# One level of Strassen in both float32 feed-forward products of two token groups, up and down as separate phases

## The chip, the cores and the metric

One core of one Trainium2 chip runs the whole layer. The metric is the device time of one execution in microseconds (us), as the median over runs. The engines are called as in the profile: PE (matmuls; PEld loads its weights), DVE (VectorE), ACT (ScalarE), POOL (GpSimd) and SP, which issues the DMAs here.

## The reference

One layer of a streaming encoder over 1024 prompt rows and 64 sample rows, width 1024, hidden width 4096, all in float32. Cut to what matters:

```python
u2 = x1 * (1.0 + sc2) + sh2
f = jnp.square(jax.nn.relu(u2 @ w['w_up'] + w['b_up'])) @ w['w_down'] + w['b_down']
y = _ln(ALPHA * x1 + (1.0 + g2) * f, w['ln2_g'], w['ln2_b'])
```

Ahead of it stand a conditioned input product, a recurrence, a band attention, an output product and LN1, which gives `x1`.

## The kernel before

The 1088 rows (tokens) are the columns of all tiles, in three groups of 384, 384 and 320. A float32 product is made of three matmuls (`mm3`, L101): each operand is split into a high part, which ACT copies out, and a low part, which DVE subtracts (`wsplit` L83 for weights, `split` L93 for activations); the three are high by high, high by low, low by high. The program has these stages in order: the conditioning and the input `u`; eight heads; the output product and LN1 with the activations `u2h`, `u2l` of each group (L526 to L592); the feed-forward and LN2 (L594 to L710).

The feed-forward goes in eight chunks of four blocks of 128 hidden columns (f-blocks). `up` (L617) loads and splits one 512 KB weight block and makes the three groups' hidden tiles: 24 matmuls a group, `relu` and square on ACT (L607, L608), high and low part on DVE (L609, L610), in SBUF. `down` (L625) takes the four f-blocks of the chunk for one group: eight output blocks of 12 matmuls, and one DVE operation each that adds the PSUM result into `facc` (L635), which lies in SBUF for all groups and was begun in LN1 by POOL (L576). In the last chunk `final` (L637) of a group comes right behind its `down`: transposes back to rows, statistics, normalisation on ACT (L650), multiplication by `lg` on DVE (L652), addition of `lb` on POOL (L653), and the output (L654).

The order of each engine's instructions is set by a scheduler that works from the program's order and a timeline it keeps itself; each engine then runs its own list in order. All DMAs are issued by SP, in its order, and one that waits for a buffer holds those behind it. The weights' raw and split tiles (`wraw`, `whi`, `wlo`) have three buffers each.

Of the kernel before, what the change touches and what calls it, by code (L numbers as in the profile page):

```python
# [47 lines left out]
def body(nc, tc, a):  # L48
    V, S, G, TE, SY = nc.vector, nc.scalar, nc.gpsimd, nc.tensor, nc.sync
    with ExitStack() as es:  # L50
        cpool = es.enter_context(tc.tile_pool(name="const", bufs=1))
# [49 lines left out]
        def mm3(ps, wh, wl, xh, xl, first, last):  # L101
            TE.matmul(ps, wh, xh, start=first, stop=False)  # L102
            TE.matmul(ps, wh, xl, start=False, stop=False)  # L103
            TE.matmul(ps, wl, xh, start=False, stop=last)  # L104

        # ------------------------------------------------ conditioning and u
# [454 lines left out]
        def ln1_b(g, n1, c, cw):  # L561
# [11 lines left out]
            for fb in range(NB):  # L573
                if fb not in facc:
                    facc[fb] = big([P, T], f"facc{fb}")
                G.tensor_scalar(facc[fb][:, t0 + c:t0 + c + cw], nT[:, fb, :], sA[:, fb:fb + 1], bA[:, fb, w:w + 1],  # L576
                                op0=ALU.mult, op1=ALU.add)
# [34 lines left out]
        def up_w(f):  # L612
            return wsplit(a["w_up"][f], f"u{f}")
# [163 lines left out]
```

## Time and profile before

| | us |
|---|---|
| median of three runs (1808.9 to 1810.18) | 1809.67 |
| span of the profiled execution, first to last instruction (the page has no other time of it) | 1807.1 |
| PE busy, 11032 matmuls | 1771.4 |
| DVE busy | 888.7 |
| ACT busy | 611.9 |
| POOL busy | 167.4 |

Times count from the start of the span. Busy times of different engines lie beside each other; a group of instructions has a total, a mean in ns and, behind the bar, the idle time that its engine had just before them, with what ended it. Matmuls are pipelined, so one lasts longer in its row than the distance to the next.

### The profile page before, as it was taken

The page shows a single profiled execution, that of the slowest core. Times are in us where ns is not written, and L with a number is a line of the kernel's source. Part 1 is how long each engine was busy: PE and PEld are TensorE (multiplying, and loading weights), DVE is VectorE, ACT ScalarE, POOL GpSimd, SP SyncE. Part 2 cuts the span into 40 slices and gives each one's busy share as a digit, 9 for nine tenths or more (in the row PEclk, how much of TensorE's full clock was granted, in tenths as well). Part 3 has the DMA queues.
Part 4 walks back from the last instruction along what each step waited for, and adds up shares of the span by engine and source line. Part 5 has one row for each costly group of instructions (what it writes and reads, how often), then busy time and mean ns, then how long its engine had stood idle before and what let it go on. Part 6 is the DMA issues. An engine that isn't in the chain of part 4 may idle for free.

```text
span 1807.1 us, 26471 instructions
## 1 busy us (share of the span) xinstructions
PE 1771.4 (98%) x11032; PEld 1738.7 (96%) x11032; DVE 888.7 (49%) x1707; ACT 611.9 (34%) x981; POOL 167.4 (9%) x243
## 2 busy tenths in 40 slices
PE   7999999999999999999999999999999999999995
PEld 4999999999999999999999999999999999999995
DVE  5594553637455374653657742424242434333447
ACT  2452534526244362533534531313130312121232
POOL 1100010000001000010027620000000000000004
PEclk9999999999999999999999999999999999999998
DMA  9231213112121212212264220202020202020102
GB/s 363 92 119 57 96 55 105 54 61 92 67 98 49 91 62 72 77 67 76 79 192 150 66 71 12 82 12 83 12 80 15 70 24 71 15 69 24 57 15 99
DMA packets 50711, 137.84 MB, mean 76 GB/s; under 512 B 6752, under 2 KB 18272, under 8 KB 50592
## 3 DMA queue, kind: packets, MB, share of 16 engines
q1 hardware_dynamic: 50592, 136.16, 22.0%
q8 instruction: 86, 1.41, 0.3%
q14 instruction: 33, 0.27, 0.0%
HBM read 123.03 MB, written 13.11 MB: 75 GB/s over the span
## 4 chain that ended last, share of the span: by engine, by line
PE 94%; DVE 2%; POOL 2%; DMA 1%; issue 1%; ACT 0%; SPq 0%; ACTq 0%; POOLq 0%; DVEq 0%
PE z L104 12%; PE z L103 12%; PE z L102 12%; PE up L104 7%; PE up L102 7%; PE up L103 7%; PE dn L102 7%; PE dn L104 7%; PE dn L103 7%; PE po L395 3%; PE s L384 2%; PE pt L389 1%; PE op L104 1%; PE op L102 1%; PE op L103 1%; POOL facc L576 1%
## 5 line engine op out<-in xcount | busy, mean ns | idle before, releaser
L102 PE MATMUL z<-uh,wh_in 128*128 128x384 f32 (+1 forms) x1320 | 435.5, 330 | 2.9 <-ACT uh L95 2.9
L103 PE MATMUL z<-ul,wh_in 128*128 128x384 f32 (+1 forms) x1320 | 436.8, 331 | 0.3 <-DVE ul L96 0.3
L104 PE MATMUL z<-uh,wl_in 128*128 128x384 f32 (+1 forms) x1320 | 435.7, 330 | 0.0
L635 DVE SCALAR_TENSOR_TENSOR facc<-dn,ada,facc 128x384 f32<-128x384 f32 (+2 forms) x256 | 122.1, 498 | 310.2 <-PE dn L104 310.1
L102 PE MATMUL dn<-hh,wh_d 128*128 128x384 f32 (+1 forms) x768 | 253.9, 331 | 3.8 <-DVE facc L635 3.7
L102 PEld LDWEIGHTS z<-uh,wh_in 128*128 128x128 f32 x1320 | 248.7, 188 | 6.3 <-ACT uh L95 3.9
L102 PE MATMUL up<-u2h,wh_u 128*128 128x384 f32 (+1 forms) x768 | 251.1, 328 | 2.0 <-ACT u2h L95 2.0
L103 PEld LDWEIGHTS z<-ul,wh_in 128*128 128x128 f32 x1320 | 248.6, 188 | 4.4 <-DVE ul L96 2.3
L104 PEld LDWEIGHTS z<-uh,wl_in 128*128 128x128 f32 x1320 | 248.5, 188 | 4.0 <-issue 3.1
L104 PE MATMUL dn<-hh,wl_d 128*128 128x384 f32 (+1 forms) x768 | 251.8, 328 | 0.0
L103 PE MATMUL dn<-hl,wh_d 128*128 128x384 f32 (+1 forms) x768 | 251.7, 328 | 0.0
L103 PE MATMUL up<-u2l,wh_u 128*128 128x384 f32 (+1 forms) x768 | 251.3, 328 | 0.0
L104 PE MATMUL up<-u2h,wl_u 128*128 128x384 f32 (+1 forms) x768 | 244.3, 328 | 0.0
L607 ACT ACTIVATE h<-up,bup 128x384 f32<-128x384 f32 (+1 forms) x96 | 53.4, 556 | 356.3 <-PE up L104 356.3
L102 PEld LDWEIGHTS dn<-hh,wh_d 128*128 128x128 f32 x768 | 144.1, 188 | 5.0 <-DVE facc L635 4.3
L102 PEld LDWEIGHTS up<-u2h,wh_u 128*128 128x128 f32 x768 | 144.5, 188 | 2.3 <-ACT u2h L95 2.3
L104 PEld LDWEIGHTS up<-u2h,wl_u 128*128 128x128 f32 x768 | 144.0, 188 | 1.4 <-DVE wl_u L90 1.4
L103 PEld LDWEIGHTS up<-u2l,wh_u 128*128 128x128 f32 x768 | 144.8, 188 | 0.0
L103 PEld LDWEIGHTS dn<-hl,wh_d 128*128 128x128 f32 x768 | 144.4, 188 | 0.0
L104 PEld LDWEIGHTS dn<-hh,wl_d 128*128 128x128 f32 x768 | 144.2, 188 | 0.0
L89 ACT ACTIVATE wh_in<-wr_in 128x1024 fp32r<-128x1024 f32 x56 | 59.4, 1060 | 105.2 <-PE z L103 100.3
L90 DVE TENSOR_TENSOR wl_in<-wr_in,wh_in 128x1024 fp32r<-128x1024 f32 x56 | 68.5, 1223 | 43.2 <-ACT wh_in L89 43.0
(237 smaller groups left out, 2379.2 us busy)
## 6 DMA issues: line engine op xcount, KB each, us to landing
wr_in<-in_w_in SPq DMA_DIRECT2D x56, 512.0 KB, 3.3
ar<-in_w_ada SPq DMA_DIRECT2D x46, 512.0 KB, 5.0
wr_u<-in_w_up SPq DMA_DIRECT2D x33, 512.0 KB, 3.3
wr_d<-in_w_down SPq DMA_DIRECT2D x32, 512.0 KB, 3.9
wr_o<-in_w_out SPq DMA_DIRECT2D x24, 512.0 KB, 3.3
xT<-in_xT SPq DMA_DIRECT2D x8, 544.0 KB, 8.7
out_y<-y SPq DMA_DIRECT2D x8, 512.0 KB, 2.6
mg_d<-gl SPq DMA_DIRECT2D x7, 544.0 KB, 2.7
```

Of the source, the lines that this page charges most:

```text
L89: S.activation(hi, raw, AF.Copy)
L90: V.tensor_tensor(lo, raw, hi.bitcast(F32), op=ALU.subtract)
L102: TE.matmul(ps, wh, xh, start=first, stop=False)
L103: TE.matmul(ps, wh, xl, start=False, stop=False)
L104: TE.matmul(ps, wl, xh, start=False, stop=last)
L384: TE.matmul(sps[:, bk, :cw], qq[:, q0:q0 + P], kk[:, P * j0 + c0:P * j0 + c0 + cw], start=(ip == 0), stop=(ip == 2))
L389: TE.transpose(pt[:, P * j:P * j + P] if j < 4 else po[:, P:2 * P], pr[:, P * j:P * j + P], ident)
L395: TE.matmul(po[:, :P], v[:, j0 + j, :], pts[:, P * j:P * j + P], start=(j == 0), stop=(j == nk - 1))
L576: G.tensor_scalar(facc[fb][:, t0 + c:t0 + c + cw], nT[:, fb, :], sA[:, fb:fb + 1], bA[:, fb, w:w + 1], op0=ALU.mult, op1=ALU.add)
L607: S.activation(h1[:, :tw], ps[:, :tw], AF.Relu, bias=bup[:, f:f + 1])
L635: V.scalar_tensor_tensor(fc, ps[:, c0:c1], ada[:, G2, fb, w:w + 1], fc, op0=ALU.mult, op1=ALU.add)
```

## The change

The 2x2 block form of a product (two row halves of the weights' output, two halves of the contraction, groups 0 and 1 as the two column halves) takes seven products of quarter size in place of eight, with sums of weights and sums of activations as operands. An f-block is paired with the one four further on, 16 pairs in all.

The first two pairs are still made plainly, during LN1 of group 2. For pairs 2 to 15 `wops` loads both weight blocks, makes four sums of 128x512 on POOL and splits the blocks and the sums; `strassen` makes 84 matmuls of 128x384 for the seven products, with each of the three PSUM tiles x, y, z shared by products; `after` adds the tiles up on DVE and applies relu and square on ACT. The activation sums T1 to T4 are made once, on DVE. Group 2 stays plain (`up_g2`); for the last four pairs it is made behind all the Strassen products, with the weights loaded again. `put_pair` makes four sums of each pair's hidden tiles on POOL and writes seven operands to DRAM (`hs_d`), and group 2's tiles go to `hg_d`. The start of `facc` goes to `facc_d` in DRAM, from LN1.

The down phase then has, for each of four chunks, seven operands of 128x1536 (786 KB) loaded (two raw buffers) and split, and four blocks of two output blocks each, 84 matmuls, whose seven products go straight from PSUM into `facc` on DVE. Behind it stand group 2's down products in two halves (r = 0 and 1) of four output blocks, with the weights loaded again, `final` of groups 0 and 1 between the halves, and `final` of group 2 at the end. `w_down` lies in another layout in DRAM.

The diff, cut to its core:

```diff
-        fs = range(c, c + CH)
...
-            for g in range(3):
-                down(fs, ws, g)
-                if c == NFF - CH:
-                    final(g)
+        def put_pair(p, c11, c12, c21, c22, g2s, new_t):
+            c, i = divmod(p, 4)
+            t1, t2, t3, t4 = (new_t(f"t{p}_{k}") for k in range(4))
+            G.tensor_tensor(t1, c12, c11, op=ALU.subtract)
+            G.tensor_tensor(t2, c22, t1, op=ALU.subtract)
+            G.tensor_tensor(t3, c22, c12, op=ALU.subtract)
+            G.tensor_tensor(t4, c21, t2, op=ALU.subtract)
+            for k, src in enumerate((c11, c21, t2, t1, t3, c22, t4)):
+                SY.dma_start(hs_d[c, k][:, i, :], src)
...
+        for q in range(2):
+            k2 = slice(2 * q, 2 * q + 2)
+            x, y, z = (fp.tile([P, 2, GW], F32, tag="tt", bufs=3, name=f"tt{q}_{k}") for k in range(3))
...
+            join(x, b11)
+            join(y, b12)
+            join(z, b22)
+            V.tensor_tensor(x, y, x, op=ALU.subtract)
+            V.tensor_tensor(y, z, y, op=ALU.subtract)
+            V.tensor_tensor(z, z, x, op=ALU.subtract)
+            tsplit(2, z)
+            tsplit(1, x)
+            join(x, b21)
+            tsplit(3, y)
+            V.tensor_tensor(x, x, z, op=ALU.subtract)
+            tsplit(4, x)
+        uops = [b11, b21, ut[2], ut[1], ut[3], b22, ut[4]]
...
+            split(*wa, ra)
+            G.tensor_tensor(s1, rb[:, h[0], :], rb[:, h[1], :], op=ALU.add)
+            G.tensor_tensor(s2, s1, ra[:, h[0], :], op=ALU.subtract)
+            split(*sums[0], sr[0])
+            G.tensor_tensor(s3, ra[:, h[0], :], rb[:, h[0], :], op=ALU.subtract)
+            G.tensor_tensor(s4, ra[:, h[1], :], s2, op=ALU.subtract)
+            split(*sums[1], sr[1])
...
+            x, z, y = acc(f"x{nm}"), acc(f"z{nm}"), acc(f"y{nm}")
+            for k, (ps, more) in enumerate(((x, False), (z, False), (x, True), (y, False), (x, True), (y, True), (x, True))):
+                for kb in range(4):
+                    mm3(ps[:, :GW], w[k][0][:, kb, :], w[k][1][:, kb, :], m[k][0][:, kb, :], m[k][1][:, kb, :],
+                        kb == 0 and not more, kb == 3, more)
+                after(k, ps[:, :GW])
...
+        for c in range(4):
+            ops = []
+            for k in range(7):
+                o = hp.tile([P, 4, GW], F32, tag="opr", bufs=2, name=f"op{c}_{k}")
+                SY.dma_start(o, hs_d[c, k])
+                ops.append(op_split(o, f"{c}_{k}"))
+            for j in range(4):
...
+                w, wa, wb = wops(a["w_down"][c, 2 * j], a["w_down"][c, 2 * j + 1], f"d{c}_{j}", False)
...
+                    for b, g in {0: [(0, 0)], 1: [(0, 0)], 2: [(0, 1)], 3: [(1, 1)], 4: [(1, 1)], 5: [(0, 1)], 6: [(1, 0)]}[k]:
+                        fb = 2 * j + b
+                        fc = facc[fb][:, GW * g:GW * g + GW]
+                        V.scalar_tensor_tensor(fc, ps, ada[:, G2, fb, 0:1], fc, op0=ALU.mult, op1=ALU.add)
...
+        fg = actb.tile([P, NB, TW2], F32, tag="act", bufs=2, name="fg")
+        SY.dma_start(fg, facc_d[:, :, TS2:T])
...
+        for r in range(2):
+            ps = [acc(f"dg{4 * r + b}") for b in range(4)]
+            for c in range(4):
+                for h in range(2):
+                    o = hp.tile([P, 4, TW2], F32, tag="opr", bufs=2, name=f"hg{r}_{c}_{h}")
+                    SY.dma_start(o, hg_d[:, 8 * c + 4 * h:8 * c + 4 * h + 4, :])
+                    hg[h] = op_split(o, f"g{r}_{c}_{h}")
+                for b in range(4):
+                    wh, wl = wsplit(a["w_down"][c, 4 * r + b], f"dg{r}_{c}_{b}")
...
+            if r == 0:
+                final(0)
+                final(1)
+        final(2)
```

How the order of the engines' instructions changes is shown at three places. The numbers at the ends of names only number the buffers.

The first place is DVE where the early f-blocks end. In the names, `hh3` and `hl3` are the hidden tile's parts, `wl_d0` a low part of a down weight; before, the row of instructions was:

```order
L90 TENSOR_TENSOR wl_d0_9923<-wr_d0_9920,wh_d0_9922 128x1024
L609 CAST hh3_9623<-h1_3_1_9759 128x384
L96 TENSOR_TENSOR u2l2_9374<-uf2_256_9775,u2h2_9373 128x8x64
L610 TENSOR_TENSOR hl3_9624<-h1_3_1_9759,hh3_9623 128x384
L90 TENSOR_TENSOR wl_d1_9929<-wr_d1_9926,wh_d1_9928 128x1024
L90 TENSOR_TENSOR wl_u0_9887<-wr_u0_9884,wh_u0_9886 128x1024
L609 CAST hh3_9623<-h1_3_2_9819 128x320
```

Now the hidden tiles' splits are gone; `wlo_u3_0` is the low part of pair 3's first weight block, `tt0_*` are the raw sums of the first half of T1 to T4, `zu2` a PSUM tile and `slo_u2_0` the low part of pair 2's weight sums:

```order
L103 TENSOR_TENSOR wlo_u3_0_10191<-wr_u3_0_10180,whi_u3_0_10190 128x1024
L689 TENSOR_TENSOR tt0_0_9938<-u2h0_8497,u2l0_8498 128x768
L689 TENSOR_TENSOR tt0_1_9939<-u2h1_8933,u2l1_8934 128x768
L689 TENSOR_TENSOR tt0_2_9940<-u2h1_8933,u2l1_8934 128x768
L697 TENSOR_TENSOR tt0_0_9938<-tt0_1_9939,tt0_0_9938 128x768
L774 TENSOR_TENSOR c2_0_10002<-zu2_10007,c2_0_10002 128x384
L698 TENSOR_TENSOR tt0_1_9939<-tt0_2_9940,tt0_1_9939 128x768
L103 TENSOR_TENSOR T1l_9933<-tt0_0_9938,T1h_9932 128x768
L699 TENSOR_TENSOR tt0_2_9940<-tt0_2_9940,tt0_0_9938 128x768
L103 TENSOR_TENSOR slo_u2_0_9982<-sr_u2_0_9980,shi_u2_0_9981 128x1024
L689 TENSOR_TENSOR tt0_0_9938<-u2h0_8497,u2l0_8498 128x768
L103 TENSOR_TENSOR T3l_9935<-tt0_1_9939,T3h_9934 128x768
```

The whole of the T operands stands behind `wlo_u3_0`, and goes on with the second half to row `T4l` 17 rows further.

The second place is SP. Before, at a border of two chunks (`wr_u` up and `wr_d` down weight blocks):

```order
L85 DMA wr_d20_13660<-in_w_down 128x1024
L85 DMA wr_d21_13666<-in_w_down 128x1024
L85 DMA wr_d22_13672<-in_w_down 128x1024
L85 DMA wr_d23_13678<-in_w_down 128x1024
L85 DMA wr_u24_14016<-in_w_up 128x1024
L85 DMA wr_u25_14114<-in_w_up 128x1024
L85 DMA wr_u26_14212<-in_w_up 128x1024
```

Now, at the border of the two phases (`cg15_*` are group 2's last hidden tiles, `op0_*` the operands of the down phase's first chunk, `fg` and `lgb` the tiles of group 2's `facc` and of LN2's two rows):

```order
L636 DMA hg_d_89<-cg15_0_12847 128x320
L834 DMA fg_14993<-facc_d_87 128x8x320
L837 DMA lgb_14995<-in_ln2 128x1024
L636 DMA hg_d_89<-cg15_1_12876 128x320
L815 DMA op0_0_12889<-hs_d_88 128x1536
L815 DMA op0_1_12895<-hs_d_88 128x1536
L821 DMA facc0_12931<-facc_d_87 128x768
...
L713 DMA wr_d0_11_13061<-in_w_down 128x1024
...
L713 DMA wr_d0_20_13183<-in_w_down 128x1024
L815 DMA op0_2_12901<-hs_d_88 128x1536
```

Loads of activations and of `facc` now stand in SP's list with the weights, `op0_0` behind `fg`, and `op0_2` behind eight `facc` loads.

The third place is DVE where `final` of groups 0 and 1 stands. Before (`y0_*` are the rows of group 0, `dn28_1_*` PSUM results of group 1), it stood between evictions of `down`:

```order
L635 SCALAR_TENSOR_TENSOR facc1_8697<-dn28_1_0_15370,ada_78,facc1_8697 128x384
L516 SCALAR_TENSOR_TENSOR lmvb0_256_15358<-lmvb0_256_15358 128x1
L652 TENSOR_TENSOR y0_0_15302<-y0_0_15302,lg_15180 128x1024
L635 SCALAR_TENSOR_TENSOR facc3_8701<-dn28_1_2_15397,ada_78,facc3_8701 128x384
L652 TENSOR_TENSOR y0_128_15328<-y0_128_15328,lg_15180 128x1024
L652 TENSOR_TENSOR y0_256_15354<-y0_256_15354,lg_15180 128x1024
L635 SCALAR_TENSOR_TENSOR facc4_8703<-dn28_1_4_15424,ada_78,facc4_8703 128x384
L635 SCALAR_TENSOR_TENSOR facc6_8707<-dn28_1_6_15451,ada_78,facc6_8707 128x384
```

Now (`wl_dg1_0_*` are the low parts of the second half's first weight blocks):

```order
L859 TENSOR_TENSOR y0_256_15600<-y0_256_15600,lgb_14995 128x1024
L519 BN_AGGR lmvb1_256_15682<-lstb1_256_15681 128x2
L523 SCALAR_TENSOR_TENSOR lmvb1_0_15630<-lmvb1_0_15630 128x1
L521 TENSOR_SCALAR lmvb1_256_15682<-lmvb1_256_15682 128x1
L859 TENSOR_TENSOR y1_0_15626<-y1_0_15626,lgb_14995 128x1024
L97 TENSOR_TENSOR wl_dg1_0_1_15743<-wr_dg1_0_1_15740,wh_dg1_0_1_15742 128x1024
L523 SCALAR_TENSOR_TENSOR lmvb1_128_15656<-lmvb1_128_15656 128x1
L523 SCALAR_TENSOR_TENSOR lmvb1_256_15682<-lmvb1_256_15682 128x1
L859 TENSOR_TENSOR y1_128_15652<-y1_128_15652,lgb_14995 128x1024
L859 TENSOR_TENSOR y1_256_15678<-y1_256_15678,lgb_14995 128x1024
L97 TENSOR_TENSOR wl_dg1_0_2_15773<-wr_dg1_0_2_15770,wh_dg1_0_2_15772 128x1024
L97 TENSOR_TENSOR wl_dg1_0_3_15803<-wr_dg1_0_3_15800,wh_dg1_0_3_15802 128x1024
```

Multiplications by `lg` stand ahead of the weights that the next matmuls take.

## Rows read from the trace of the kernel before

**Rows 1.** The page's busy times: share of the span, number of instructions.
```profile
PE 1771.4 (98%) x11032; PEld 1738.7 (96%) x11032; DVE 888.7 (49%) x1707; ACT 611.9 (34%) x981; POOL 167.4 (9%) x243
```
**Rows 2.** The page's chain that ended last, by engine.
```profile
PE 94%; DVE 2%; POOL 2%; DMA 1%; issue 1%; ACT 0%; SPq 0%; ACTq 0%; POOLq 0%; DVEq 0%
```
**Rows 3.** Busy time by stretch: length, engines (instructions), granted clock, DMA share, GB/s.
```profile
1062.00:1740.00 678.00, 678.00 (x4094) 676.57 (x4093) 243.71 (x457) 146.28 (x229) 0.00 (x0) 1.00 0.14 45
```
**Rows 4.** PE's waits from 1062 us on: total us, times, longest.
```profile
PE dn L102 <- DVE facc L635: 3.7, 2, 3.0
```
**Rows 5.** Timeline of PE: start, us, line, operation, tiles.
```profile
1092.14 0.34 PE L102 MATMUL dn<-hh,wh_d 128*128 128x384 f32 x1
...
1094.24 0.31 PE L102 MATMUL up<-u2h,wh_u 128*128 128x320 f32 x1
...
1096.00 0.34 PE L102 MATMUL dn<-hh,wh_d 128*128 128x384 f32 x1
```
**Rows 6.** POOL's groups by shape: count, total, mean ns.
```profile
L653 POOL TENSOR_TENSOR y<-y,lb 128x1024 f32<-128x1024 f32 x6 | 15.1, 2525 | 7.9 <-issue 3.4 <-DVE y L652 2.4 <-PE dn L104 2.0
...
L323 POOL TENSOR_TENSOR ko<-kh,kl 128x512 f32<-128x512 f32 x8 | 10.3, 1290 | 212.5 <-DVE kl L317 182.1 <-DVE kc L319 30.5
```
**Rows 7.** Timelines of DVE and of POOL in `final` of group 0.
```profile
1758.04 1.23 DVE L652 TENSOR_TENSOR y<-y,lg 128x1024 f32<-128x1024 f32 x1
...
1759.96 4.05 DVE L652 TENSOR_TENSOR y<-y,lg 128x1024 f32<-128x1024 f32 x2
1763.93 1.13 DVE L635 SCALAR_TENSOR_TENSOR facc<-dn,ada,facc 128x384 f32<-128x384 f32 x2
...
1759.40 2.40 POOL L653 TENSOR_TENSOR y<-y,lb 128x1024 f32<-128x1024 f32 x1 [2.04 <-PE dn L104]
1763.02 5.58 POOL L653 TENSOR_TENSOR y<-y,lb 128x1024 f32<-128x1024 f32 x2 [1.22 <-DVE y L652]
```
**Rows 8.** Busy time by stretch, columns as in rows 3, where loads are densest.
```profile
30.00:40.00 10.00, 9.26 (x63) 7.58 (x64) 7.45 (x19) 4.05 (x10) 4.84 (x4) 1.00 1.04 411
```
**Rows 9.** DVE's groups by shape from 1062 us on.
```profile
L635 DVE SCALAR_TENSOR_TENSOR facc<-dn,ada,facc 128x384 f32<-128x384 f32 x128 | 78.8, 617 | 199.3 <-PE dn L104 199.3
...
L90 DVE TENSOR_TENSOR wl_u<-wr_u,wh_u 128x1024 fp32r<-128x1024 f32 x28 | 33.7, 1222 | 25.3 <-ACT wh_u L89 25.3
...
L610 DVE TENSOR_TENSOR hl<-h,hh 128x384 fp32r<-128x384 f32 x56 | 30.7, 557 | 1.5
...
L511 DVE BATCH_NORM_STATS2 lstb<-y 128x6 f32<-128x512 f32 x12 | 8.0, 682 | 5.2 <-ACT y L667 4.9
```
**Rows 10.** The page's DMA issues: count, KB each, median us to landing.
```profile
wr_d<-in_w_down SPq DMA_DIRECT2D x32, 512.0 KB, 3.9
```
**Rows 11.** SP's waits from 940 us on.
```profile
SPq L85 <- DVE hh L609: 346.3, 31, 36.9
```
**Rows 12.** ACT's groups by shape from 940 us on.
```profile
L89 ACT ACTIVATE wh_u<-wr_u 128x1024 fp32r<-128x1024 f32 x33 | 34.2, 1054 | 100.4 <-PE up L103 99.3 <-PE op L103 1.2
...
L608 ACT ACTIVATE h<-h 128x384 f32<-128x384 f32 x64 | 33.6, 525 | 1.9
...
L650 ACT ACTIVATE y<-y,lmvb 128x512 f32<-128x512 f32 x12 | 8.7, 804 | 5.3 <-DVE lmvb L516 3.2 <-DVE lmvb L514 2.1
...
L667 ACT ACTIVATE y<-yt 128x512 f32<-128x512 f32 x12 | 6.8, 599 | 27.7 <-PE yt L663 17.7 <-DMA out_y<-y 10.0
```
**Rows 13.** The page's GB/s in 40 equal slices of the span.
```profile
GB/s 363 92 119 57 96 55 105 54 61 92 67 98 49 91 62 72 77 67 76 79 192 150 66 71 12 82 12 83 12 80 15 70 24 71 15 69 24 57 15 99
```
**Rows 14.** Busy time of PE by stretch near the start: granted clock, DMA share, GB/s.
```profile
10.00:15.00 5.00, 1.45 (x10) 1.00 1.02 410
15.00:20.00 5.00, 4.06 (x10) 0.50 1.03 417
20.00:25.00 5.00, 5.00 (x22) 0.82 1.02 413
```

More of the change, by code (lines that the diff above doesn't have):

```diff
@@ L25 @@
 GW = 384
+TW2 = 320
+TS2 = 2 * GW
 NFF = 32
-CH = 4
 BAND = 512
@@ L99, in split, with mm3 @@
                 V.scalar_tensor_tensor(lo, src, scl, hi.bitcast(F32), op0=ALU.mult, op1=ALU.subtract)
[L101 to L104, printed above, removed]
+        def mm3(ps, wh, wl, xh, xl, first, last, more=False):
+            TE.matmul(ps, wh, xh, start=first, stop=False, skip_group_check=more)
+            TE.matmul(ps, wh, xl, start=False, stop=False, skip_group_check=more)
+            TE.matmul(ps, wl, xh, start=False, stop=last, skip_group_check=more)
         SY.dma_start(csb, a["c"])
@@ L573, in ln1_b @@
             for fb in range(NB):
[L574 to L577, printed above, removed]
+                G.tensor_scalar(nT[:, fb, :], nT[:, fb, :], sA[:, fb:fb + 1], bA[:, fb, w:w + 1], op0=ALU.mult, op1=ALU.add)
+            SY.dma_start(facc_d[:, :, t0 + c:t0 + c + cw], nT)
         def ln1(g, rT, fill):
@@ new lines, in body, with early @@
+        wt = {}
+        ef = (*fblocks(0), *fblocks(1))
+        def early(i):
+            for f in (ef[0:2], (), ef[2:4], ())[i] if i < 4 else ():
+                wt[f] = up_w(f)
+                up_mm(f, wt[f], 0)
+            for f in ((), ef[0:2], (), ef[2:4])[i] if i < 4 else ():
+                up_mm(f, wt[f], 1)
+        ln1(2, rTs[2], early)
+        for f in ef[:0:-1]:
+            up_mm(f, wt[f], 2)
+        up_mm(ef[0], up_w(ef[0]), 2)
+        for p in range(2):
+            h1, h2 = (hraw[f] for f in fblocks(p))
+            put_pair(p, h1[:, 0:GW], h1[:, GW:TS2], h2[:, 0:GW], h2[:, GW:TS2], [h1[:, TS2:T], h2[:, TS2:T]],
+                     lambda nm: big([P, GW], nm))
@@ new lines, in body, with acc, whole @@
+        tok_es.close()
+        fp = up_es.enter_context(tc.tile_pool(name="fp", bufs=1, side="right", reuse_waits="tile"))
+        psp = up_es.enter_context(tc.tile_pool(name="psp3", bufs=1, space=PSUM, reuse_waits="tile"))
+        spool = [fp]
+        def acc(nm):
+            return psp.tile([P, 512], F32, tag="acc", bufs=8, name=nm)
+        def whole(x):
+            return x.bitcast(F32)
+        ut = {}
+        for k in (2, 1, 3, 4):
+            ut[k] = (fp.tile([P, 4, GW], R32, tag=f"t{k}h", name=f"T{k}h"), fp.tile([P, 4, GW], R32, tag=f"t{k}l", name=f"T{k}l"))
@@ new lines, in body, with op_split @@
+        for p in range(2, 16):
+            up_pair(p)
+        for p in range(LATE, 16):
+            up_g2(p, *(up_w(f) for f in fblocks(p)))
+        up_es.close()
+        hp = es.enter_context(tc.tile_pool(name="hp", bufs=1, reuse_waits="tile"))
+        psp = es.enter_context(tc.tile_pool(name="psp4", bufs=1, space=PSUM, reuse_waits="tile"))
+        spool[0] = hp
+        facc = {}
+        def op_split(src, nm):
+            hl = [hp.tile(list(src.shape), R32, tag=t, bufs=7, name=f"{t}{nm}") for t in ("oph", "opl")]
+            split(*hl, src)
+            return hl
```

204 lines of the change are left out of this document (129 added, 75 removed).

## The prediction

> **What bounds the kernel now.** I read the page's busy shares first: TensorE (PE) is busy for 1771.4 of 1807.1 us, VectorE (DVE) for 888.7, ScalarE (ACT) for 611.9, GpSimd (POOL) for 167.4 [rows 1]. The chain that ended last says the same: 94% of it is PE [rows 2]. Busy time by stretches then tells where the feed-forward stands: from 1062 to 1740 us PE is busy for all of 678.00 us, DVE for 243.71, POOL for none, and DMA moves 45 GB/s [rows 3]. In the waits of PE after 1062 us nothing is left but 3.7 us [rows 4]. So the stage that is changed is a row of matmuls back to back, every one of them costs its pitch, and anything that stops PE there is a new loss. The pitch comes from the timeline: 12 matmuls of 128x384 take 1092.14 to 1094.24, 0.175 us each; 12 of 128x320 take 1094.24 to 1096.00, 0.147 us each [rows 5]. The profiled span is 1807.1 us, the median of the runs 1809.67: 2.6 us lie around the span, and I add them unchanged.
>
> **What is saved.** A 2x2 block product of groups 0 and 1 is 8 quarter products of 12 matmuls (4 blocks of 128, three matmuls each) before and 7 after. Up has 14 such pairs, down 16 (4 chunks of 4): 30 x 12 = 360 matmuls of 128x384 less, 360 x 0.1745 (2.094 over 12, before rounding) = **-62.8 us**. Nothing of 320 columns goes. The order shows these counts, so that the change does less than it says is excluded. Before LN1 the order is the same.
>
> **What is added, and covers itself.** In the steady up phase a pair keeps PE busy for 84 x 0.1745 + 48 x 0.147 = 21.7 us. POOL does eight subtractions and sums: 128x512 took 1.29 and 128x1024 2.40 us [rows 6, 7], so I estimate 2.17 ns per element, 1.01 for 128x384, together 9.2 us. ACT has four splits of 1.054 and 15 passes of 0.525 over one group [rows 12], some 12 us, DVE four residuals of 1.222 and three additions of 0.617 [rows 9], 6.7. Nothing there exceeds PE; the writes of h to DRAM (9 per pair, 1.7 MB) take 4 us of the queue at 411 GB/s [rows 8]. I cost it at nothing; cover is PE's 21.7 us. In pairs 12 to 15 without group 2, PE has 14.7 us and the two vector engines together 13.6: +1.5 (0 to 3).
>
> **The entry of the up phase.** Operands T1 to T4 are made on DVE: 16 operations and 8 residuals of 128x768. DVE took 0.557 us for 384 and 1.222 for 1024 elements [rows 9], so I estimate 0.956 for 768: 22.9 us. Among them stand three weight residuals (3.7) and a 0.6 us addition: 27 us. The order puts the chain behind `wlo_u3_0` of pair 3, whose weights are issued on SP behind `hs_d<-t`, that is behind POOL; with landing (3.9 us for such a block [rows 10]) and split the chain starts some 4.5 us after the first four f-blocks are done, and with half of four POOL sums (5.2 us) in its way it ends 36 us after. PE has 74 x 0.1745 + 48 x 0.147 = 19.9 us of work until the product that needs the end. **+16** (12 without POOL, 20 with all of it).
>
> **From up to down.** At the end of the last up block, T1, SP stands at `fg<-facc_d`, whose buffer the last matmul frees. Behind it in the same queue: `fg` 1.31 MB, `lgb` 2 x 0.52, a small write, `op0_0`, `op0_1` (0.79 each), eight `facc` (0.39 each), two weight blocks, then `op0_2`: 9.1 MB in all. That a queue in order holds all behind a wait is the present kernel's habit (346.3 us of SP waits there, harmless since the weights are early [rows 11]). At 411 GB/s [rows 8] that is 22.1 us. The split of 128x1536 takes ACT 1.5 (0.525 for 384, 1.054 for 1024 [rows 12]) and DVE 1.75 [rows 9]. So `op0_2` is ready at T1 + 26 (rounded up by the issue), and PE has only 24 matmuls, 4.2 us, before. **+22**: 18 if the split is half hidden, 27 at 363 GB/s, the rate of the first slice of the page [rows 13].
>
> **The steady down phase.** A block is 84 matmuls, 14.66 us of PE. DVE: a residual 1.22, two of the sums 2.45, a half one 0.69, seven evictions of 0.617 [rows 9], 8.7; a quarter of seven operand residuals adds 3.1: 11.8. POOL's four sums are 5.16. What they do to each other is seen at the end of before: DVE's multiplication of 128x1024 takes 1.23 alone; started at 1759.96 beside POOL's addition (1759.40, 2.40 us) two of them take 4.05, 1.84 of it until POOL ends at 1761.80 and 2.21 for both; the evictions from PSUM run on beside POOL (1763.93, two in 1.13) [rows 7]. [...] If half of POOL's time stops DVE, a block is 14.4 of 14.66: it just holds. At the three borders of chunks seven operand residuals (12.3 us) fall into about one block, since only two raw buffers and seven split ones are there: some 3 us each. **+10**, from 0 to 30 (nearly all of POOL's time on DVE).
>
> **Group 2's second half.** Before, `final` of groups 0 and 1 ran beside the down matmuls of the next group, whose weights were there. Now the six tiles (12 ACT copies of 0.599, 12 normalisations of 0.804 [rows 12], 12 statistics of 0.682, six multiplications [rows 9], six POOL additions of 2.525 [rows 6]) stand on DVE, ACT and SP before the second weight block of r=1, and the third and fourth weights are issued behind outputs that wait for POOL. Statistics end 8 us after the transposes; four multiplications with three additions between them end at some 22; then come blocks of 24 x 0.147 = 3.5 us. PE works for 3.5 of the first 23 us and waits again for the fourth: **+20** (11 if three additions are hidden, 24 with all).
>
> **The clock.** [...] Four idle stretches come; in two of them PE afterwards waits for data anyhow: **+6** (3 to 12). `facc_d` writes in LN1 and the tail I cost at nothing: the tail is the same work, and the writes are 4.5 MB over some 100 us.
>
> **Sum.** -62.8 + 16 + 1.5 + 22 + 10 + 20 + 6 = +12.7: 1807.1 + 12.7 = 1819.8 of span, with 2.6 around it **1822**. All lower ends give -62.8 + 44 = 1791, all upper ends 1863. Its own range: 1807 to 1838.
>
> **Rivals.** *DVE keeps ahead.* Place: DVE's queue at the borders of chunks and in r=1. If DVE's blocks with POOL beside it stay under 14.66 us even with operand residuals, and PE's reserve of weights (three buffers) covers three additions of `final`, the terms 10, 20, 6, 1.5 become 0, 11, 3, 0: -62.8 + 52 = -10.8, **1799**; its point is those 14.66 us. For it: sums are made a block ahead. Against it: 14.4 is nearly 14.66, and SP's queue puts three outputs ahead. If the two transitions lose some 15 us as well, as they would where transfers already stand in the buffers, 1784.
> [...] If all of POOL's 5.16 stops DVE, a block takes 11.8 + 5.2 = 17.0, 2.3 over PE's 14.66, over 16 blocks 36 in place of 10: **1848**. [...] For it: the row where DVE waits for the whole rest of POOL's addition; against it: evictions do not wait.
>
> **How the numbers follow.** The forecast has 0.52, DVE ahead 0.30, the port 0.18. 0.2% (3.6 us) is about what a measurement of this kernel can tell. The forecast lies within it for about 0.10, below for 0.02; of DVE ahead 0.02 is within. Faster 0.30, same 0.12, slower 0.58. The range, 1784 to 1850, takes in the rivals and leaves out about 0.15 at the ends of both.
>
> **What would show it.** PE's waits should have four places: one of 12 to 20 us on DVE at the entry of up (T, `slo_u2`), one at the border to down whose last part is `op0_2`, small ones per chunk, and one in r=1 behind `wl_dg1_0`. Pitches should stay 0.175 and 0.147, the clock dip after the long idle times, and POOL show some 220 us more (64 of 1.01, 120 of 1.29). [...]

## The result and the profile after

The changed kernel takes **1832.33 us** (median of four runs, 1831.26 to 1833.49), the kernel before 1809.72 beside it: ratio 1.0128, 95% interval 1.0113 to 1.0142. It is slower by 1.3%, as forecast, and 10 us later than the predicted 1822, inside the range of 1784 to 1850. The profiled execution took 1832.08 us with a span of 1830.3.

The page's busy times of the changed kernel, and its chain by engine, answer to [rows 1, 2]:

```profile
PE 1733.1 (95%) x10672; PEld 1689.0 (92%) x10672; DVE 1038.6 (57%) x1597; ACT 785.8 (43%) x1175; POOL 438.6 (24%) x427
...
PE 84%; DVE 5%; DMA 4%; issue 3%; ACT 3%; POOL 1%; SPq 0%; ACTq 0%; DVEq 0%; POOLq 0%
```

The 360 matmuls are gone (11032 to 10672), PE's busy time fell by 38 us, and the span grew by 23: what was saved came back as idle time of PE (35.7 us before, 97.2 now) and as slower matmuls. The chain that was 94% PE is 84% PE now, and DVE, DMA and ACT have 12%. The six longest waits of PE from 1062 us on [rows 4 for before] (total us, times, longest):

```profile
PE xd L109 <- ACT oph L102: 18.6, 2, 13.2
PE yu L109 <- ACT shi_u L102: 11.2, 13, 6.1
PE dg L109 <- ACT wh_dg L96: 9.7, 3, 6.0
PE dg L111 <- DVE wl_dg L97: 7.8, 3, 3.2
PE xu L109 <- ACT c L772: 3.8, 2, 1.9
PE xu L110 <- DVE T2l L103: 2.4, 1, 2.4
```

`xd` is the border of the two phases, `dg` group 2's second half, `yu` and `xu` the up phase. Three places can be seen as dips in PE by stretch (length, PE busy, granted clock, DMA share, GB/s): the entry of up, the border, and the second half.

```profile
1080.00:1090.00 10.00, 8.38 (x41) 0.68 0.07 23
1090.00:1100.00 10.00, 8.62 (x51) 1.00 0.00 0
1100.00:1110.00 10.00, 5.87 (x18) 0.67 0.42 138
...
1410.00:1420.00 10.00, 0.26 (x1) 0.53 1.03 387
1420.00:1430.00 10.00, 7.53 (x24) 0.62 1.04 407
1430.00:1440.00 10.00, 4.92 (x14) 0.55 0.89 338
...
1730.00:1740.00 10.00, 3.87 (x17) 0.74 0.29 103
1740.00:1750.00 10.00, 3.60 (x15) 0.67 0.26 105
1750.00:1760.00 10.00, 5.92 (x24) 0.67 0.64 211
```

At the border DMA is full or nearly so for 30 us (387, 407 and 338 GB/s) while PE stands: data is late there. At the entry DMA moves next to nothing before 1100, and in the second half it is a quarter to two thirds busy, so that another engine is late. The granted clock falls at each of the three.

I measured each term as PE's time over the pitch (start to start of neighbouring matmuls of one shape), stretch by stretch. Gaps of more than 0.35 us over the pitch count as idle; what the pitch itself grows by counts to the clock. T0, the first Strassen matmul, is at 1071.2 us, T1, the end of up, at 1406.4, the last `dg` matmul at 1812.4. Before, the same early matmuls end at 1064.8, and 2.7 us of that went to ten down matmuls among them, which leaves 1062.1.

| term | predicted | measured |
|---|---|---|
| matmuls saved | -62.8 | -62.8 |
| LN1, up to T0 (1062.1 before) | 0 | 9.1 |
| entry of up, idle | 16 | 12.7 |
| steady up | 0 | 3.1 |
| last four pairs | 1.5 | 10.9 |
| border to down, idle | 22 | 22.1 |
| steady down | 10 | 0.3 |
| group 2's second half, idle | 20 | 18.7 |
| clock (with some 2.4 of transposes in the second half) | 6 | 19.2 |

These give +33.3. The terms are whole losses of the changed kernel. By the same count the kernel before lost some 10 us itself after 1062 (3.7 of them waits [rows 4], some 3 its own transposes), which come off; that leaves the 23.2 us between the spans.

### The profile page after: what moved, and what is told of

Its sections match the earlier page's. It is cut to its first block, busy times and chain, and to the rows that moved or that the text cites. A ratio compares the mean times of both kernels' runs of the same rounds, so it can differ in the third digit from the quotient of the medians.

```text
span 1830.3 us, 26877 instructions
## 1 busy us (share of the span) xinstructions
PE 1733.1 (95%) x10672; PEld 1689.0 (92%) x10672; DVE 1038.6 (57%) x1597; ACT 785.8 (43%) x1175; POOL 438.6 (24%) x427
## 4 chain that ended last, share of the span: by engine, by line
PE 84%; DVE 5%; DMA 4%; issue 3%; ACT 3%; POOL 1%; SPq 0%; ACTq 0%; DVEq 0%; POOLq 0%
PE z L110 12%; PE z L111 12%; PE z L109 12%; PE po L402 3%; PE s L391 2%; PE xu L109 2%; PE xu L110 2%; PE dg L111 2%; PE dg L110 2%; PE dg L109 2%; PE xd L110 2%; PE xd L109 2%; PE xd L111 2%; PE xu L111 2%; PE ug L109 2%
## 5 line engine op out<-in xcount | busy, mean ns | idle before, releaser
L109 PE MATMUL dg<-ophg,wh_dg 128*128 128x320 f32 x256 | 82.1, 321 | 9.7 <-ACT wh_dg L96 9.7
L111 PE MATMUL dg<-ophg,wl_dg 128*128 128x320 f32 x256 | 82.4, 322 | 7.8 <-DVE wl_dg L97 7.8
L110 PE MATMUL dg<-oplg,wh_dg 128*128 128x320 f32 x256 | 81.6, 319 | 0.0
L160 DVE SCALAR_TENSOR_TENSOR ap<-ar,sil,ap 128x512 f32<-128x512 f32 x112 | 79.8, 744 | 0.0
L103 DVE TENSOR_TENSOR opl<-op,oph 128x1536 fp32r<-128x1536 f32 x28 | 58.5, 2091 | 24.5 <-ACT oph L102 24.3
L103 DVE TENSOR_TENSOR wlo_u<-wr_u,whi_u 128x1024 fp32r<-128x1024 f32 (+1 forms) x28 | 47.9, 1737 | 40.0 <-ACT whi_u L102 40.0
L374 ACT ACTIVATE pr<-pr,st 128x640 f32<-128x640 f32 (+2 forms) x64 | 44.7, 699 | 57.7 <-DVE st L373 57.5
L402 PE MATMUL po<-pts,v 128*128 128x128 f32 x480 | 64.1, 275 | 0.5 <-ACT pts L398 0.3
L102 ACT ACTIVATE oph<-op 128x1536 fp32r<-128x1536 f32 x28 | 41.6, 1487 | 50.6 <-DMA op<-hs_d 45.9
L402 PEld LDWEIGHTS po<-pts,v 128*128 128x128 f32 x480 | 61.2, 191 | 1.2 <-ACT pts L398 1.2
```

Of the source, the lines that this page charges most:

```text
L102: S.activation(hi, src, AF.Copy)
L103: V.tensor_tensor(lo, src, hi.bitcast(F32), op=ALU.subtract)
L109: TE.matmul(ps, wh, xh, start=first, stop=False, skip_group_check=more)
L110: TE.matmul(ps, wh, xl, start=False, stop=False, skip_group_check=more)
L111: TE.matmul(ps, wl, xh, start=False, stop=last, skip_group_check=more)
L160: V.scalar_tensor_tensor(part[:, w, :], raw[:, j, :], sil[:, kb, w:w + 1], part[:, w, :], op0=ALU.mult, op1=ALU.add)
```

## The experiments

The first four ran on one chip, where the kernel before took 1806.84 in one run. A time without an interval is that of a single run. Since the first 60 us vary by some 3 us between the profiled runs (the 100th matmul starts at 59.1 to 62.0), stretches are compared as well as totals.

**Group 2's second half.** `final` of groups 0 and 1 moves into the second half, behind its first weights, and its rows lie in the buffers of the weight sums, no longer in the weights':

```diff
-                y = wp.tile([P, D], F32, tag=("whi", "wlo", "wraw")[c // P], name=f"y{g}_{c}")
+                y = hp.tile([P, D], F32, tag=("shi", "slo", "sraw")[c // P], bufs=2, name=f"y{g}_{c}")
...
+                if r == 1 and c < 2:
+                    final(c)
...
-            if r == 0:
-                final(0)
-                final(1)
```

> Edit: the second half of group 2's down products starts at once, final of group 0 stands behind its first four weight blocks and final of group 1 behind its next four; the row tiles y of these two groups lie in the weight sums' buffers, not in the weights' own. Theory (five places give the saving back, each by itself): PE's 27.8 us of loss between 1725 and 1770 us fall to about 5 (the transposes and a little), so 1832.3 becomes 1806 to 1814. Rival (ACT, DVE and POOL together are the limit there, the wait only spreads over the half): the loss stays above 18 us, 1823 or more.

It took 1817.38 us; from the end of down to the last `dg` matmul 119.1 us in place of 139.2. PE's waits from 1720 us on are down to one row:

```profile
PE dg L111 <- DVE wl_dg L97: 3.8, 1, 3.8
```

The total misses the expected 1806 to 1814, because the end of up came 4.1 us later in this run; the 20 us of this place are gone. They came from `final` standing ahead of weights or from its rows in the weights' buffers: the edit changes both, and no run separates them.

**The border.** `fg`, `lgb` and six of the eight `facc` loads go behind the operands on SP:

```diff
-                        SY.dma_start(facc[fb], facc_d[:, fb, 0:TS2])
+                        with tc.issue_after(opl[1 if fb < 2 else 6]):
+                            SY.dma_start(facc[fb], facc_d[:, fb, 0:TS2])
```

(`fg` and `lgb` alike, behind the ninth operand load.)

> Edit: the loads of fg, lgb and of six of the eight facc tiles are issued on SP behind the first chunk's operand loads. Theory (the queue's order makes the border's wait): op0_2 then has 3.4 MB ahead of it in place of 8.3 MB, and nothing waits for the last up matmul but one small write; PE's 27.5 us of loss at the border fall to 12 to 17, 1832.3 becomes 1818 to 1822. Rival (the operands' splits and the memory of the up phase set the border, the bytes do not): the loss stays at 24 or more, 1829 or more.

1825.3 us; T1 to the last `dg` matmul 398.2 in place of 406.1: 7.9 us won, less than expected. Two of PE's waits there, in the timeline:

```profile
1415.90 0.69 PE L109 MATMUL xd<-oph,whi_d 128*128 128x384 f32 x1 [8.21 <-ACT oph L102]
...
1426.81 0.45 PE L109 MATMUL xd<-oph,shi_d 128*128 128x384 f32 x1 [1.92 <-ACT oph L102]
```

The order of these loads makes some 7.6 of the border's 22.1 us of idle time. 14.5 stay, 8.2 of them at once: `op0_0` still stands on SP behind the write of group 2's last hidden tile, which ACT makes after the last up matmul. PE has no other work in that time.

**The last four pairs.** `LATE`, the pair from which group 2 is made at the end, goes from 12 to 16, so that every pair keeps its plain work.

```diff
-        LATE = 12
+        LATE = 16
```

> Edit: group 2's up products of the last four pairs stand with their pairs, as in the pairs before, and eight weight loads fall away. Theory (a pair without group 2 has nothing to run while ACT copies the first PSUM tile out and the sums are split, 10.9 us in the last stretch): these 10.9 fall to 1 to 3, the border stays at 25 to 29, so 1822 to 1826. Rival (the late products cover loads of the border): the border grows by 8 or more and the time stays at 1830 to 1836.

1819.74 us; T0 to T1 326.8 in place of 335.2. The 8.4 us, of the 10.9 there, belong to pairs without plain work. The total lies below the expected 1822 to 1826, since T0 came 4.7 us earlier in this run.

**LN1: the sums on POOL.** The eight sums of the first two pairs are issued behind LN1's last POOL operation (`tail`):

```diff
+            with tc.issue_after(tail[0].ins):
                 put_pair(p, h1[:, 0:GW], h1[:, GW:TS2], h2[:, 0:GW], h2[:, GW:TS2], [h1[:, TS2:T], h2[:, TS2:T]],
```

> Edit: POOL's eight sums of the first two pairs' hidden tiles stand behind its last work for LN1. Theory (in LN1's last tile POOL's new work delays the statistics and so the last matmuls of the first four f-blocks, 9.1 us later than before): if these sums are the cause, 5 to 9 us come back, 1823 to 1828. Rival (the delay comes from the start of facc, which POOL now makes in place, behind DVE's reading of the same tile): at most 2 us come back, 1830 to 1833.

1830.8 us. From the last out-projection matmul to T0 it takes 61.1 us, 62.8 in the changed kernel (62.5 to 63.9 in those of its variants that leave this stretch alone), 56.9 to the same point before. These sums are a small part at most.

**Filling the entry and the border.** Each pair from the fourth on keeps one of its two plain blocks of group 2; five blocks go ahead of the first pair, eight behind the last, their writes issued by ACT:

```diff
-        LATE = 12
+        ENTRY = [(3, 1), (4, 1), (5, 1), (6, 1), (7, 1)]
+        END = [(8, 1), (9, 1), (10, 1), (11, 1), (12, 1), (13, 1), (14, 1), (15, 1)]
```

> Edit: no pair is without group 2 any more; from pair 3 on only the first of a pair's two f-blocks has its group-2 product with the pair, the other one is made elsewhere: those of pairs 3 to 7 at the entry of the up phase, while the T operands are made, those of pairs 8 to 15 behind the last pair, and their writes to DRAM are issued by ACT. Theory (the entry and the last four pairs lose because PE has no plain work beside a chain of DVE, ACT and POOL): the entry's loss of 17.4 us falls to 3 to 9 and the last pairs' 10.9 to 1 to 4, the border stays at 22 to 28, so the time from the first Strassen matmul to the end of the up phase plus the five blocks moved ahead of it is 12 to 22 us less, in all about 1811 to 1820. Rival (the five weight blocks ahead delay the T operands by as much as PE gains): the entry's loss stays above 13, 1823 or more.

1845.39 us: missed; the rival's total came, but not for its reason. The entry's idle time fell to some 2 us, but every pair now loses 3.0: they follow each other by 21.2 us, for 18.2 of work. Two of PE's waits from 1062 us on:

```profile
PE yu L109 <- ACT shi_u L102: 13.2, 14, 1.0
PE xu L111 <- DVE wlo_u L103: 11.9, 12, 1.0
```

A pair needs both plain blocks beside it; a block that is taken from every pair costs in every pair more than it can cover at the ends.

**POOL's sums twice in down.** Each of the four sums of the down phase is made two times:

```diff
+            for _ in range(2 if nm[0] == "d" else 1):
+                G.tensor_tensor(s1, rb[:, h[0], :], rb[:, h[1], :], op=ALU.add)
+                G.tensor_tensor(s2, s1, ra[:, h[0], :], op=ALU.subtract)
...
```

> Edit: POOL makes each of the four sums of weights of a down block twice (64 more sums of 128x512, the same values). The prediction's third case, and half of it its forecast, let POOL's 5.16 us a block stop DVE: then 5.16 more a block bring DVE from near 14.4 past PE's 14.66 and the down phase grows by 20 to 60 us (2 to 4 a block). Theory (DVE has 8 to 10 us of work a block, and POOL takes its gaps): it grows by less than 6 us.

1875.58 us; the down phase takes 294.2 in place of 253.6. My theory was wrong: the 64 further sums are 82.6 us at 1.29 [rows 6], and 40.6, half of that, reaches the path. The long waits stand at the three borders of chunks (8.2, 6.8 and 7.6 us), the first of them here:

```profile
1512.57 0.69 PE L109 MATMUL xd<-oph,whi_d 128*128 128x384 f32 x1 [8.20 <-ACT whi_d L102]
```

That is the place that the prediction named, but not its reason, DVE held up by POOL. Busy times over the down phase (length, PE, PEld, DVE, ACT, POOL, granted clock, DMA share, GB/s), in the changed kernel and in this run:

```profile
1419.74:1673.48 253.74, 245.78 (x1376) 242.82 (x1377) 207.11 (x208) 106.36 (x97) 98.02 (x60) 0.96 0.52 180
...
1419.43:1713.82 294.39, 256.59 (x1376) 249.12 (x1377) 215.75 (x207) 103.08 (x95) 217.48 (x120) 0.92 0.44 153
```

POOL works 119.5 us more, DVE only 8.6. Ahead of the first long wait DVE stands idle, as its operand is loaded late:

```profile
1499.73 1.29 POOL L730 TENSOR_TENSOR sr_d<-wr_d,sr_d 128x512 f32<-128x512 f32 x1
...
1499.80 1.58 SPq L713 DMA_DIRECT2D wr_d<-in_w_down  x2
1501.48 11.28 SPq L817 DMA_DIRECT2D op<-hs_d  x3
...
1509.14 1.48 ACT L102 ACTIVATE oph<-op 128x1536 fp32r<-128x1536 f32 x1 [14.03 <-DMA op<-hs_d]
...
1510.66 1.76 DVE L103 TENSOR_TENSOR opl<-op,oph 128x1536 fp32r<-128x1536 f32 x1 [10.43 <-ACT oph L102]
```

POOL frees the raw weight buffers late (between 1420 and 1700 us the weights' loads on SP wait 92 us for its sums, 38 from 1420 to 1680 in the changed kernel), the operand's load stands on SP behind these loads, and ACT, DVE and PE wait for that operand. So the down phase holds with one set of sums and not with two; how much POOL could do beside one set no run shows.

**LN1: the start of facc.** LN1's multiply-adds write a tile of their own in place of overwriting `nT`:

```diff
+            fT = big([P, NB, cw], f"fT{g}_{c}")
...
-                G.tensor_scalar(nT[:, fb, :], nT[:, fb, :], sA[:, fb:fb + 1], bA[:, fb, w:w + 1], op0=ALU.mult, op1=ALU.add)
+                G.tensor_scalar(fT[:, fb, :], nT[:, fb, :], sA[:, fb:fb + 1], bA[:, fb, w:w + 1], op0=ALU.mult, op1=ALU.add)
```

> Edit: in LN1 POOL writes the start of facc into a tile of its own in place of the tile that DVE reads (that tile is written to DRAM then). From the first out-projection matmul to the first Strassen matmul it was 139.4 us, and 131.8 before for the same matmuls. Theory (made in place, POOL's work has to wait for DVE's reading of the tile and then stands before the next tile's statistics): 132 to 135. Rival (the writes to DRAM and the sums of the hidden tiles on POOL delay it): 137 or more.

1837.11 us, and 65.4 in LN1's stretch: not the cause.

**All three places covered.** The edits of the second half, the border and the filling stand together, with the eight end blocks issued behind the first chunk's operand loads, and that chunk's later weights split behind the operands.

> Edit: the group-2 products moved as in the run e6_entry_fill, those behind the last pair stand behind the first chunk's operand loads and splits in the program; the loads of fg, lgb and six facc tiles stand behind the operand loads, the first chunk's later weights are split behind the operands; final of groups 0 and 1 as in the run e2_final_mid. Theory (each place gives back its own loss and nothing else binds): of 17.4 + 10.9 + 27.5 + 27.8 us of loss some 15 to 25 are left, so 1765 to 1780, faster than before by 1.5 to 2.5%. Rival (with the gaps closed, DVE, ACT or the transfers bind in their place): 1790 or more.

1804.89 us (nine runs), before 1810.01, ratio 0.9977 (0.9967 to 0.9987): faster than both kernels, but far from the 1765 to 1780 expected. PE no longer stands at the border itself, with 3.3 us of idle time in the block behind it, and T1 to the last `dg` matmul takes 362.2 in place of 406.1. What is left is mainly the loss in each pair, some 3 us as in the run before, and the rival's number came.

**LN1: statistics first.** POOL's multiply-adds are issued behind the power operation of the latest statistics (`powi`):

```diff
+            with tc.issue_after(powi[-1]):
+                for fb in range(NB):
+                    tail[0] = G.tensor_scalar(nT[:, fb, :], nT[:, fb, :], sA[:, fb:fb + 1], bA[:, fb, w:w + 1], op0=ALU.mult, op1=ALU.add)
```

> One edit to the changed kernel: in the first layer norm, POOL's eight multiply-adds on nT of a tile are issued behind POOL's power operation on the next tile's statistics, so that the last tile's statistics no longer stand behind them (5.05 us in the changed kernel's trace, at 1042). Theory (the 62.8 us from the last out-projection matmul to the first half-size one, against 56.9 in the kernel before, come from that place in POOL's queue): 58 to 60 here. Rival (they come from the slower copies and adds around it, and the statistics were not what was late): 62 or more, total within 2 us of the changed kernel's 1832.

1834.45 us, 62.1 in the stretch: the rival holds. The statistics came earlier on POOL (1043.55 us in place of 1047.19), but PE takes its transposes at the same place in its order.

**Whole pairs, together and apart.** Two kernels start from the one with all places covered and have the edits of sums behind and statistics first. They differ only in which pairs give away both plain blocks (bare pairs):

```diff
-        ENTRY = [(11, 0), (11, 1), (12, 0), (12, 1)]
-        END = [(13, 0), (13, 1), (14, 0), (14, 1), (15, 0), (15, 1)]
+        ENTRY = [(4, 0), (4, 1), (6, 0), (6, 1)]
+        END = [(8, 0), (8, 1), (10, 0), (10, 1), (12, 0), (12, 1)]
```

> The combination that was faster than both, with other blocks moved: instead of one plain group-2 block from each of eleven pairs, both blocks of five pairs (11 and 12 to the entry of the first phase, 13 to 15 to the end of that phase), and the power operation of the layer norm ahead of its multiply-adds. Theory (a pair without any plain work costs about 2.6 us, one with half of it 2.4, so fewer bare pairs cost less): the stretch from the first half-size matmul to the last of the first phase is shorter by some 10 to 14 us than in the combination once the blocks moved ahead of it are counted, total 1785 to 1797. Rival (neighbouring bare pairs run dry together, as the last four of the changed kernel do): 5 us or less is won, total 1800 or more.

> As the run with whole pairs, but the bare pairs stand apart: 4 and 6 give their plain blocks to the entry, 8, 10 and 12 to the end. Theory (the loss belongs to the pair: its t sums are ready late whatever stands beside it): within 3 us of the run with whole pairs. Rival (the plain work of the neighbours lets DVE and POOL run ahead and covers it): another 5 to 10 us less than that run.

Together 1798.32 us, ratio 0.9936 (0.9921 to 0.995); apart 1778.76, ratio 0.9826 (0.9809 to 0.9842). The first falls between its theory and its rival, the second goes beyond its rival: what a bare pair costs depends on its neighbours. PE's waits from 1110 us to the end of up, with the bare pairs together:

```profile
PE xu L109 <- ACT c L779: 8.0, 4, 2.4
PE yu L109 <- ACT shi_u L102: 6.5, 12, 1.5
```

The same view with the bare pairs apart:

```profile
PE yu L109 <- ACT shi_u L102: 7.0, 8, 1.6
```

Two neighbouring bare pairs follow each other by 18.05 us (1325.57 to 1343.62) for 14.66 of work, 3.4 lost in each; a bare and a whole pair take 37.67 together (1148.91 to 1186.58) for 36.36, 1.3 lost. The 8.0 us of waiting on `c` are gone where pairs stand apart (0.6 us on another `c` stand in both). The bare pairs also differ in their place, 11 to 15 against 4 to 12, which no run tells apart from their distance.

**LN1: PE's order.** On the kernel with pairs apart, one early block waits for the transposes `nt` of group 1's last tile, and another is kept for the time behind those of group 2's:

```diff
-                up_mm(f, wt[f], 0)
-            for f in ((), ef[0:2], (), ef[2:4])[i] if i < 4 else ():
-                up_mm(f, wt[f], 1)
+                with tc.issue_after(ntl[0].ins) if f == ef[1] else ExitStack():
+                    up_mm(f, wt[f], 0)
+            for f in ((), ef[0:2], (), ef[2:3], ef[3:4])[i]:
+                with tc.issue_after(ntl[0].ins) if i == 4 else ExitStack():
+                    up_mm(f, wt[f], 1)
```

> As the run with alternating pairs, and in the first layer norm 48 early matmuls change their place on PE: the second early block waits for the transposes nt of group 1's last tile (which stand behind 24 of these matmuls, 11 in the kernel before, 41 in the changed one), and one block of group 1 is kept for the time behind nt of group 2's last tile, where the kernel before has ten down matmuls and the changed one nothing. Theory (the 5 to 6 us that the layer norm takes longer than in the kernel before, from the last out-projection matmul to the end of the early blocks, come from PE's order, since the two waits of 2.3 and 3.5 to 4.9 us there stand right behind these transposes): 61.5 becomes 56 to 58, the total 1773 to 1776. Rival (the tiles are late on DVE, POOL or ACT, and a wait moved goes elsewhere): 60 or more, total 1777 to 1781.

**1770.5 us**, ratio 0.9794 (0.9778 to 0.981), the fastest here and faster than expected; the stretch is 54.3 us in place of 61.5, shorter than the 56.9 of the kernel before. Its two changes were not tried apart. PE's timeline at group 2's last tile, in the kernel before:

```profile
1044.00 0.71 PE L566 MATMUL nt<-ident,n 64*128 64x64 f32 x8
1044.63 0.44 PE L102 MATMUL dn<-hh,wh_d 128*128 128x384 f32 x1
...
1047.98 0.71 PE L102 MATMUL up<-u2h,wh_u 128*128 128x320 f32 x3 [1.97 <-ACT u2h L95]
```

The same place in the changed kernel:

```profile
1050.02 0.71 PE L572 MATMUL nt<-ident,n 64*128 64x64 f32 x8 [1.03 <-ACT n L564]
1055.40 1.17 PE L109 MATMUL up<-u2h,wh_u 128*128 128x320 f32 x3 [4.67 <-ACT u2h L102]
```

And in this run:

```profile
1042.09 0.71 PE L576 MATMUL nt<-ident,n 64*128 64x64 f32 x8 [0.27 <-ACT n L568]
1042.73 0.44 PE L109 MATMUL up<-u2h,wh_u 128*128 128x384 f32 x1
```

From `nt` to the first matmul that needs `u2h` the chain over ACT, DVE and ACT takes 4.0 us before and 5.4 in the changed kernel. Before, down matmuls of the first f-blocks stand in it; the changed kernel has put all of down behind up, and PE has nothing there.

## Why the prediction was right, and where it was wrong

**Right: the sign, and the three large places.** The entry lost 12.7 us of idle time against 16, the border 22.1 against 22, the second half 18.7 against 20. Their mechanisms hold in the main too. T4's low part ended at 1106.4, 35 us after T0 (36 predicted), behind `wlo_u3_0`. SP at the border, from its timeline:

```profile
1406.40 0.59 SPq L834 DMA_DIRECT2D fg<-facc_d  x1
1407.09 0.61 SPq L837 DMA_DIRECT2D lgb<-in_ln  x1
...
1408.80 0.90 SPq L815 DMA_DIRECT2D op<-hs_d  x2
1409.74 5.26 SPq L821 DMA_DIRECT2D facc<-facc_d  x4
...
1423.10 2.66 SPq L815 DMA_DIRECT2D op<-hs_d  x2
```

`fg` is issued at T1, and the third operand behind all the rest, as read from the order. Its split by ACT starts at 1432.43, T1 + 26.0, and DVE's half ends 3 us later; the prediction had that split end at T1 + 26. So that operand was ready some 3 us later than forecast, and that the idle time agrees to 0.1 us is luck: part of the loss went to the clock, 0.53 to 0.62 over these 30 us. Edits at the instructions named then took away the second half's idle time but for 3.8 us, and a third of the border's, nearly all of it once PE had plain blocks there; the entry went by filling. PE's waits after 1062 add up to some 59 us, the third operand lands 26 us after T1, behind its queue, and the waits are not spread over the down blocks.

Three of its figures don't come out of its own terms. The chain at the entry is 4.5 + 27 + 2.6 = 34.1 us with half of the sums and 36.7 with all, not 36 and 40, so that the term is 14 with a top of 17; and the border at 363 GB/s gives 25, not 27.

**Wrong: LN1 at nothing.** The prediction says of the order before LN1 that it is the same, and has no term for LN1 but the writes of `facc_d`, at nothing. LN1's stretch lost 9.1 us. Of it 3.3 us were there at the last out-projection matmul (1008.4 against 1005.1; it came at 1004.0 to 1009.8 in the changed kernel and its variants, so that this may be scatter between runs), 5.8 behind it. What PE does while a tile's chain runs was not counted. The order shows it: group 1's last `nt` stood behind 11 early matmuls before and stands behind 41 now, and the ten down matmuls at group 2's last tile are gone. The last run put matmuls back at both places and won 7.2 us of the stretch, more than the 5.8; three edits on POOL's side won 1.7 at most or lost.

**Wrong: last four pairs, 1.5 for 10.9.** The step was "PE has 14.7 us and the two vector engines together 13.6". Busy sums don't bound it; a loop does. One of the four pairs, ACT in the changed kernel's timeline:

```profile
1334.38 0.63 ACT L102 ACTIVATE whi_u<-wr_u 128x512 fp32r<-128x512 f32 x1 [1.86 <-PE xu L110]
1334.92 0.56 ACT L608 ACTIVATE c<-xu,bup 128x384 f32<-128x384 f32 x1
1335.39 1.05 ACT L102 ACTIVATE whi_u<-wr_u 128x1024 fp32r<-128x1024 f32 x1
1336.33 0.51 ACT L609 ACTIVATE c<-c 128x384 f32<-128x384 f32 x1
1336.74 0.48 ACT L772 ACTIVATE c<-xu 128x384 f32<-128x384 f32 x1
```

PE and POOL beside it:

```profile
1337.28 0.44 PE L109 MATMUL xu<-T2h,shi_u 128*128 128x384 f32 x1 [1.88 <-ACT c L772]
...
1332.80 1.29 POOL L727 TENSOR_TENSOR sr_u<-wr_u,wr_u 128x512 f32<-128x512 f32 x1 [6.22 <-DVE slo_u L103]
```

ACT waits for PE to free a weight buffer, splits into it, and only behind that copies `xu` out of PSUM, for which PE's next product waits; POOL idles 6.22 us for a buffer of the sums. The pairs follow each other by 18.0 us, not 14.66. That this loop from buffer to buffer is what bounds them is read from the timeline; no run changed the number of buffers. Plain matmuls beside the pair take the loss away, as the run without late pairs shows (8.4 of 10.9 us), and those of a neighbour take some of it, by the runs with pairs together and apart.

**Wrong: steady down, 10 for 0.3.** The step was that half of POOL's 5.16 us stops DVE, which puts a block at 14.4 of 14.66 and leaves no room for the operand residuals at the borders of chunks. DVE was busy for 207.1 us in the 16 blocks, 12.9 a block, its longer operations included (the residuals of 128x1024 took 1.31 us for the sums and 1.80 for the weights in the mean, 1.22 before [rows 9]), and the operand residuals fit into the rest. The run with the sums twice doesn't bear the step out either, though half of the added time reached the path: there POOL's own work delays the weights' buffers and the loads behind them. POOL's work did take longer: its busy time grew by 271 us in the changed kernel, where the prediction expected 220; the sums of the down phase took 1.36 to 1.98 us in the mean, 1.29 alone [rows 6].

**Wrong: the clock, 6 for some 17**, without the transposes. The 6 was my estimate, and no run shows it; what the runs show is that more stretches fell, and for longer, than in the rows of before [rows 14]. At the border matmuls of 384 columns follow each other by 0.32 us from 1422.02 to 1425.22, where the granted clock is 0.50, and by 0.17 from 1427.78 to 1428.30, where it is back at 1.00. The second half stays at 0.67 to 0.74 over 40 us, in which PE stands six times, for 0.8 to 6.0 us.

Together: LN1 9.1, the last pairs 9.4, the clock with the transposes 13.2, steady up 3.1, the border 0.1, against 9.7 of steady down, 3.3 of the entry, 1.3 of the second half and some 10 that the kernel before lost itself; that is the 10.5 us between the predicted span, 1819.8, and 1830.3. So the total is nearer than its terms deserve: some 35 us were missing in it and some 24 too many, and that these nearly cancel is luck. Of the rival in which DVE keeps ahead one part came true, the free steady down phase; the second half and the last pairs went the other way. The third case, 1848 at 0.18, which the chances call the port, a thing that no trace shows, did not come: steady down lost 0.3 us in place of its 36.

## What to carry to other kernels

Fewer matmuls on a kernel that is bound by PE are worth what the other engines leave (62.8 us saved here, and a span longer by 23.2): ask at each border, and at each chain that ends in PE's next operand, which independent matmuls PE has meanwhile, because a change that splits work into phases takes them away. Price a steady stage by its loop through the buffers, and not by busy sums alone (18.0 us against 14.66 in the last pairs here). When a test brings the number that a mechanism asks for, look whether the engine that the mechanism names did the waiting. And cover is best taken where there is some to spare: a pair without its plain blocks cost 1.3 us here beside whole pairs, 3.4 beside others like it.

## What the hardware showed that I had not expected

An addition on POOL that takes 1.29 us alone [rows 6] lasted 11.11, from 1084.09 to 1095.20, beside eleven operations in a row on DVE. At the entry of up, POOL's timeline in the changed kernel:

```profile
1084.09 11.11 POOL L724 TENSOR_TENSOR sr_u<-wr_u 128x512 f32<-128x512 f32 x1 [6.89 <-DVE slo_u L103]
1095.28 1.90 POOL L725 TENSOR_TENSOR sr_u<-sr_u,wr_u 128x512 f32<-128x512 f32 x1
1097.13 2.00 POOL L727 TENSOR_TENSOR sr_u<-wr_u,wr_u 128x512 f32<-128x512 f32 x1
```

DVE's in the same time, the first and the last of eleven operations in a row, and what came behind:

```profile
1083.88 0.94 DVE L689 TENSOR_TENSOR tt<-u2h,u2l 128x768 f32<-128x768 f32 x1
...
1093.10 0.95 DVE L689 TENSOR_TENSOR tt<-u2h,u2l 128x768 f32<-128x768 f32 x1
1094.08 1.94 DVE L698 TENSOR_TENSOR tt<-tt,tt 128x768 f32<-128x768 f32 x1
1095.94 2.06 DVE L103 TENSOR_TENSOR T1l<-tt,T1h 128x768 fp32r<-128x768 f32 x1
```

The eleven take 0.94 to 1.21 us each, and by their rows each starts before the one ahead of it has ended. DVE's next operation starts at 1094.08, 0.03 us after the eleventh has ended, and POOL's addition ends 1.12 us later. From there the operations of both are longer while they lie beside each other: DVE's of 128x768 take 1.94 to 2.06 us for 0.95, POOL's of 128x512 1.90 to 2.00 for 1.29. What kept POOL's addition from ending earlier the trace does not show.
